# Eight steps of the conditioning product moved from the even mixer to the second feed-forward

## The chip, the cores and the metric

One Trainium2 chip, of which one core runs the kernel. The metric is the device time of one execution in microseconds (us); a kernel's time is the median of its runs. Engines: TensorE (PE, with its weight loads PEld), VectorE (DVE), ScalarE (ACT), GpSimd (POOL), SyncE (SP, which here only issues transfers).

## What is computed

One inference step of a two-layer trunk for a prompt (512 tokens) and eight samples (4 tokens each), 544 columns in all, in the model width 1024. Each layer has a feed-forward, a mixer and a second feed-forward, so there are four feed-forwards, here called first to fourth (`ffn(0)` to `ffn(3)`), an even mixer after the first and an odd mixer after the third. Each of these six parts is conditioned by a shift, a scale and a gate:

```python
mod = (jax.nn.silu(c) @ ada_w[l] + ada_b[l]).reshape(bx, 3, 3, 1, D_MODEL)   # shift, scale, gate of each part
f = _swiglu(_modulate(x, mod[:, 0]), ffn_w_gate[l, 0], ffn_w_up[l, 0], ffn_w_down[l, 0])
x = _layer_norm(ALPHA * x + 0.5 * (1.0 + mod[:, 0, 2]) * f, ln_g[l, 0], ln_b[l, 0])
def _modulate(x, m): return x * (1.0 + m[:, 1]) + m[:, 0]
def _swiglu(h, wg, wu, wd): return (jax.nn.silu(h @ wg) * (h @ wu)) @ wd
```

`ada_w` is 1024 by 9216 in fp32 for each layer. The even mixer is a differential attention of four heads beside an S5 state-space model, with a paged cache for the samples.

## The kernel before

Activations lie with the model width on partitions, 544 columns in two halves of 272. Each weight is split into two fp32r parts (`wh` by ScalarE at L448, `wl` by VectorE at L449), and a projection is three matmuls for each 128 by 128 block (L460, L461, L462).

**The conditioning product** (`ada`, L174; not touched by the diff). The 18 slots of 512 columns of `ada_w[l]` are worked out two slots (a pair, `(l, s)`) at a time, two pairs in one group. A group is eight steps, one for each 128 rows of the input. A step loads four tiles of 128 by 512 (256 KB each, SP's queue, L202) and runs four fp32 products of 32 columns of weights each, side by side in the array (L185; two records for each product, so eight). After the eighth step the result is copied to rows (ScalarE, L211), transposed (TensorE, L213) and added to the bias (VectorE, L217). `ada` is a generator: each `next` puts down one step's loads and the products of the step that lies `lag` steps back. The products are held behind the last projection matmul traced so far:

```python
with self.tc.issue_after(self.last.ins):
    first = product(3, rs[3])
...
raws[n].append(room(F32, f"h{n % 2}{18 + j}"))
```

In the feed-forwards the loaded tiles have eight slots (two steps, `lag` 2), in place of the last hidden tiles, which are not yet in use. In the even mixer they have four slots (one step, `lag` 1), in a pool of their own (`ar`), and a PSUM bank of their own (`ad`).

**A feed-forward** (`ffn`, L377): a first part of 22 hidden blocks `m`, gate and up projection for each half, Silu (L401, ScalarE), the gating multiplication (L402, VectorE) and a split; then a second part with the down projection and the normalisation. In the first part `next(ada)` is called once for each half while `2 <= m < 18` (from `m` = 4 in the first feed-forward). The `fill` argument is the list of pairs. The first feed-forward works out six pairs, the third four, the second and the fourth none.

**The even mixer** (`even_mix`, L1761): the S5 slices (`s5_slice`: products of L1055 and L1064, then of L1087, whose result `yb` and `yT` go out and come back by POOL's queue at L1090 and L1093), then for each of four heads the projections (`even_qk`; POOL copies the samples' columns at L644 and L645), the attention of the head before (`even_head`: scores L660, exponentials L664, transposes L671, copy L673, values L676) and four `next(ada)`. Then the samples' attention (`sample_attn`) in two groups of four samples: keys and values gathered by POOL from the paged cache (`sK` L698, `sV` L704, five slots together), scores L516, exponential L532, transposes L539 to L541, copies L543 and L544, values L549, and at the end a normalisation (L721). Beside it the end of the S5 part (`s5_end`: a gated projection) and the last head. The scale and the shift of a part are combined on POOL (`scale_shift`, L224), the gate too (`gate`, L219).

The order of the instructions on each engine is laid out once, when the kernel is built, by a planner that goes by the order of the program, by priorities and by its own time model; at run time each engine takes its queue in that order.

Of the kernel before, what the change touches and what calls it, by code (L numbers as in the profile page):

```python
# [9 lines left out]
F32 = mybir.dt.float32  # L10
# [16 lines left out]
class Kern:  # L27
# [1733 lines left out]
    def even_mix(self):  # L1761
        nc, D, tc = self.nc, self.D, self.tc
        es = ExitStack()
        pool = lambda n, b, **k: es.enter_context(tc.tile_pool(name=n, bufs=b, reuse_waits="tile", **k))
        self.wide(5, 1)
        self.psum(s5=1, sc=2, mm=2, ps=2, ad=1)
        with es:
            self.qz = pool("s5z", 1)
            self.cm = p1 = pool("ea1", 1)
            p2 = pool("ea2", 2)  # L1770
            q1 = pool("s5a", 1)
            q2 = pool("s5b", 3)
            self.skp = pool("sk", 5)
            pR = pool("ar", 1)
            ada = self.ada([(0, 16), (1, 0), (1, 2), (1, 4)], lambda dt, tag: pR.tile([128, 512], dt, name="ar", tag=tag[0] + tag[2:]), lambda: self.bank["ad"].tile([128, 512], F32, name="ad"), 1)
            self.cmask = self._ld(p1, "cmask")
            self.smask = self._ld(p1, "smask")
            self.o128 = p1.tile([128, 128], F32, name="o128")
            nc.gpsimd.memset(self.o128, 1.0 / 128)
            self.s5_init(q1)  # L1780
            self.even_u(q2)
            self.vt = p1.tile([128, 5, 512], F32, name="vt")
            self.qs = p1.tile([128, 4, 32], F32, name="qs")
            self.ks = p1.tile([128, 4, 32], F32, name="ks")
            self.aoT = p1.tile([128, 4, 512], F32, name="aoT")
            s5 = [self.s5_slice(d, q1, q2) for d in range(4)]
            v = self.vproj(self.vt, D["even_v"], lambda: p2.tile([128, NT], F32, name="qT"), self.ps)
            next(s5[0])
            for _ in v:
                pass  # L1790
            nc.sync.dma_start(D["a_v"][0:512].rearrange("(t p) n -> p t n", p=128), self.vt[:, 0:4])
            nc.sync.dma_start(D["a_v"][512:544], self.vt[0:32, 4])
            qk = {}
            for h in range(4):
                next(s5[h], None)
                if h < 3:
                    next(s5[h + 1])
                qk[h] = self.even_qk(h, p2)
                if h:
                    self.even_head(h - 1, *qk[h - 1], p1, p2)  # L1800
                for _ in range(4):
                    next(ada, None)
            for _ in ada:
                pass
            aos = self.even_sample(p1, p2)
            self.s5_end(q1)
            self.even_head(3, *qk[3], p1, p2)
            self.split(self.xh[:, 0:4, SP:NT], self.xl[:, 0:4, SP:NT], aos)
            for h in range(4):
                self.split(self.xh[:, h, 0:512], self.xl[:, h, 0:512], self.aoT[:, h])  # L1810

        self.psum(mm=4, ps=4)
        self.wide()
# [13 lines left out]
    def run(self):  # L1827
        nc, D = self.nc, self.D
        self.bes, pools = ExitStack(), ExitStack()
        first = self.bes.enter_context(self.tc.tile_pool(name="first", bufs=1, side="right", reuse_waits="tile"))  # L1830
        self.xh, self.xl = [first.tile([128, 8, NT], F32R, name=n) for n in ("xh0", "xl0")]
        self.pp = pools.enter_context(self.tc.tile_pool(name="pp", bufs=1, side="right", reuse_waits="tile"))
        self.s5a = self.pp.tile([128, 48], F32, name="c_s5_a")
        nc.scalar.dma_start(self.s5a, D["s5_a"])
        self.setup()
        self.ada_setup()
        self.s5hp = self.pp.tile([128, 256], F32, name="s5hp")
        nc.scalar.dma_start(self.s5hp, D["s5_par"][:, 512:768])
        gw, early = self.begin()
        self.s5_angles(pools)  # L1840
        self.ffn(0, lambda: self.gate(0, 0, 0.5), lambda: self.to_next(0, self.scale_shift(0, 1, 0)), [(0, s) for s in range(4, 16, 2)], gw, early, self.s5_matrices)
        self.mu, self.rsh = self.const("rw_mu"), self.const("rw_sh")
        xs = self.dr.tile([128, 8, NT], F32, name="xs")
        self.park(xs)
        self.even_mix()
        self.unpark(xs)
        rg = self.gate(0, 1, 1.0)
        GS = self.scale_shift(0, 2, 1)
        self.outproj(D["even_out"], rg, self.to_next(1, GS), (4, 5, 6, 7, 0, 1, 2, 3))
        self.ffn(1, lambda: self.gate(0, 2, 0.5), lambda: self.to_next(2, self.scale_shift(1, 0, 2)), ())  # L1850
        self.ffn(2, lambda: self.gate(1, 0, 0.5), lambda: self.to_next(3, self.scale_shift(1, 1, 3)), [(1, s) for s in range(6, 14, 2)])
        self.park(xs)
        self.odd_mix()
        self.unpark(xs)
        rg = self.gate(1, 1, 1.0)
        GS = self.scale_shift(1, 2, 4)
        self.outproj(D["odd_out"], rg, self.to_next(4, GS))
        self.ffn(3, lambda: self.gate(1, 2, 0.5), lambda: self.to_out(5))
        self.xes.close()
        self.wes.close()  # L1860
        self.banks.close()
# [158 lines left out]
```

## Time and profile before

| | |
|---|---|
| median of 3 runs | 2570.49 us (2568.71 to 2571.3) |
| profiled execution | 2567.64 us, span 2565.8 us |
| TensorE busy | 2442.6 us (95%) |
| VectorE, ScalarE, GpSimd busy | 1232.4, 943.3, 409.0 us |
| data moved by DMA | 318.27 MB, mean 124 GB/s |

Busy time is the time in which an engine has an instruction under way. Ends of matmuls are modelled, so a busy TensorE is not a TensorE at its peak. The granted clock is the share of TensorE's full clock (2.4 GHz) that it got; its two levels are 1.0 and 0.5 (1.2 GHz), values between are means over a stretch. The idle time in front of an instruction stands in square brackets in a timeline, with what ended it.

### The profile page before, as it was taken

The numbers are of one execution on the slowest core, as the hardware profiler recorded it, in microseconds if no ns is written. First come the engines' busy times: TensorE is split into PE (matmuls) and PEld (weight loads), VectorE is DVE, ScalarE is ACT, GpSimd is POOL, SyncE is SP. The second block draws the span as 40 slices with busy tenths as digits, with TensorE's granted clock in tenths as the row PEclk, the third lists the DMA queues.
The fourth block names the chain that finished last, engine by engine and source line by source line (L and its number), as shares of the span: only waits on it lengthen the run. The fifth ranks groups of instructions, "written<-read, shape, count | busy, mean of one in ns | idle before, by whom it ended". The sixth has DMA issues, their size and how long they took to land.

```text
span 2565.8 us, 50682 instructions
## 1 busy us (share of the span) xinstructions
PE 2442.6 (95%) x20338; PEld 2253.4 (88%) x20338; DVE 1232.4 (48%) x2999; ACT 943.3 (37%) x2051; POOL 409.0 (16%) x616
## 2 busy tenths in 40 slices
PE   6999999899899999999999999889999999999996
PEld 4988999897588999999989999878877578999996
DVE  6532356544577333345423334558664567333343
ACT  4322323435555333224323322545422545333222
POOL 1000016411432000031000003312111122000032
PEclk8999999999999999999999999889988999999998
DMA  7666335567632222223562232322322632222221
GB/s 237 203 217 216 113 118 112 188 216 252 222 122 75 87 88 94 80 80 105 173 222 83 85 91 81 103 77 78 92 75 92 211 113 74 87 89 94 80 80 58
DMA packets 184027, 318.27 MB, mean 124 GB/s; under 512 B 38416, under 2 KB 47040, under 8 KB 183664
## 3 DMA queue, kind: packets, MB, share of 16 engines
q1 hardware_dynamic: 172096, 282.52, 34.6%
q0 software_dynamic: 10400, 31.06, 4.1%
q8 instruction: 159, 2.61, 0.4%
q10 hardware_dynamic: 1296, 1.46, 0.2%
q14 instruction: 76, 0.62, 0.1%
HBM read 288.68 MB, written 26.28 MB: 123 GB/s over the span
## 4 chain that ended last, share of the span: by engine, by line
PE 82%; DVE 7%; DMA 4%; ACT 4%; issue 1%; POOL 1%; SPq 1%; ACTq 0%; POOLq 0%; DVEq 0%
PE mm L460 23%; PE mm L462 23%; PE mm L461 22%; PE ps L185 2%; DVE x L347 1%; DMA ar<-in_ada_w 1%; DMA raw<-in_ada_w 1%; ACT t L249 1%; DVE wl L449 1%; PE sc L1178 1%; PE sc L1156 1%; PE ad L185 1%; PE ps L460 1%; PE ps L462 1%; PE ps L461 1%
## 5 line engine op out<-in xcount | busy, mean ns | idle before, releaser
L460 PE MATMUL mm<-xh,wh 128*128 128x272 f32 x3720 | 1089.4, 295 | 35.5 <-ACT xh L250 10.1
L461 PE MATMUL mm<-xl,wh 128*128 128x272 f32 x3720 | 1082.7, 291 | 2.0 <-DVE xl L251 2.0
L462 PE MATMUL mm<-xh,wl 128*128 128x272 f32 x3720 | 1083.0, 292 | 0.8 <-DVE wl L449 0.8
L460 PEld LDWEIGHTS mm<-xh,wh 128*128 128x128 f32 x3720 | 706.0, 190 | 85.2 <-ACT t L401 31.2
L449 DVE TENSOR_TENSOR wl<-raw,wh 128x512 fp32r<-128x512 f32 (+1 forms) x664 | 458.8, 703 | 537.0 <-ACT wh L448 505.0
L461 PEld LDWEIGHTS mm<-xl,wh 128*128 128x128 f32 x3720 | 710.5, 191 | 7.0 <-DVE xl L251 2.5
L462 PEld LDWEIGHTS mm<-xh,wl 128*128 128x128 f32 x3720 | 706.6, 190 | 7.8 <-issue 4.2
L448 ACT ACTIVATE wh<-raw 128x512 fp32r<-128x512 f32 (+1 forms) x664 | 401.5, 618 | 727.6 <-PE mm L461 565.9
L460 PE MATMUL mm<-hh,wh 128*128 128x272 f32 x1280 | 370.4, 289 | 0.0
L462 PE MATMUL mm<-hh,wl 128*128 128x272 f32 x1280 | 370.4, 289 | 0.0
L461 PE MATMUL mm<-hl,wh 128*128 128x272 f32 x1280 | 369.5, 289 | 0.0
L460 PEld LDWEIGHTS mm<-hh,wh 128*128 128x128 f32 x1280 | 241.4, 189 | 0.8 <-issue 0.4
L461 PEld LDWEIGHTS mm<-hl,wh 128*128 128x128 f32 x1280 | 241.2, 188 | 0.4
L462 PEld LDWEIGHTS mm<-hh,wl 128*128 128x128 f32 x1280 | 241.1, 188 | 0.4
L402 DVE TENSOR_TENSOR t<-t,mm 128x272 f32<-128x272 f32 x169 | 73.4, 434 | 279.6 <-ACT t L401 279.4
L401 ACT ACTIVATE t<-mm 128x272 f32<-128x272 f32 x169 | 65.6, 388 | 318.6 <-PE mm L462 318.6
L297 POOL TENSOR_TENSOR sa<-x 128x272 f32<-128x272 f32 x24 | 26.1, 1087 | 907.4 <-DVE x L291 852.0
L291 DVE SCALAR_TENSOR_TENSOR x<-mm,rg,x 128x272 f32<-128x272 f32 (+1 forms) x96 | 45.9, 479 | 171.4 <-PE mm L462 170.7
L466 DVE TENSOR_TENSOR hl<-t,hh 128x272 fp32r<-128x272 f32 x160 | 69.6, 439 | 35.8 <-ACT hh L465 35.3
L465 ACT ACTIVATE hh<-t 128x272 fp32r<-128x272 f32 x160 | 67.5, 426 | 38.5 <-DVE t L402 38.5
L277 POOL TENSOR_TENSOR sq<-sq,t 128x272 f32<-128x272 f32 x60 | 54.7, 926 | 18.1 <-ACT t L276 17.3
L249 ACT ACTIVATE t<-x,S,G 128x272 f32<-128x272 f32 (+1 forms) x80 | 44.5, 589 | 24.1 <-DVE x L348 23.5
(643 smaller groups left out, 2536.6 us busy)
## 6 DMA issues: line engine op xcount, KB each, us to landing
raw<-in_ada_w SPq DMA_DIRECT2D x192, 256.0 KB
raw<-in_wg SPq DMA_DIRECT2D x176, 256.0 KB
raw<-in_wu SPq DMA_DIRECT2D x176, 256.0 KB
raw<-in_wd SPq DMA_DIRECT2D x160, 256.0 KB
ar<-in_ada_w SPq DMA_DIRECT2D x96, 256.0 KB
raw<-in_odd_rw SPq DMA_DIRECT2D x28, 256.0 KB
xs<-x POOLq DMA_DIRECT2D x16, 272.0 KB, 4.0
x<-xs POOLq DMA_DIRECT2D x8, 544.0 KB, 7.8
```

The costliest lines, as they stand in the source:

```text
L185: return nc.tensor.matmul(ps[32 * j:32 * j + 32], self.c32[:, 9 * k:9 * k + 32], r, start=(k == 0), stop=(k == 7))
L249: nc.scalar.activation(t[:, 0:n], x[:, d, c0:pe], AF.Identity, scale=G[:, d, 0:1], bias=S[:, d, 0:1])
L277: G.tensor_tensor(s["q"], s["q"], t, op=A)
L401: self.act = nc.scalar.activation(s, pss[2 * i], AF.Silu)
L402: mul = nc.vector.tensor_tensor(s, s, pss[2 * i + 1], op=ALU.mult)
L448: nc.scalar.activation(wh[:, 0:w], r[:, 0:w], AF.Copy)
L449: (lo or nc.vector).tensor_tensor(wl[:, 0:w], r[:, 0:w], wh[:, 0:w].bitcast(F32), op=ALU.subtract)
L460: nc.tensor.matmul(ps, wh[:, s], mh, start=first, stop=False)
L461: nc.tensor.matmul(ps, wh[:, s], ml, start=False, stop=False)
L462: self.last = nc.tensor.matmul(ps, wl[:, s], mh, start=False, stop=last)
L465: self.nc.scalar.activation(hi, src, AF.Copy)
L466: return (lo_eng or self.nc.vector).tensor_tensor(lo, src, hi.bitcast(F32), op=ALU.subtract)
```

## The change

The even mixer works out two pairs, `(0, 16)` and `(1, 0)`, in place of four, with three calls for each head in place of four. The two pairs `(1, 2)` and `(1, 4)`, the scale and the gate of the third feed-forward, are worked out in the second feed-forward's first part, which had no pairs. The tiles, slots and banks of both places stay as they are.

```diff
@@ even_mix
-            ada = self.ada([(0, 16), (1, 0), (1, 2), (1, 4)], lambda dt, tag: pR.tile(...), lambda: self.bank["ad"].tile(...), 1)
+            ada = self.ada([(0, 16), (1, 0)], lambda dt, tag: pR.tile(...), lambda: self.bank["ad"].tile(...), 1)
...
                 if h:
                     self.even_head(h - 1, *qk[h - 1], p1, p2)
-                for _ in range(4):
+                for _ in range(3):
                     next(ada, None)
@@ run
-        self.ffn(1, lambda: self.gate(0, 2, 0.5), lambda: self.to_next(2, self.scale_shift(1, 0, 2)), ())
+        self.ffn(1, lambda: self.gate(0, 2, 0.5), lambda: self.to_next(2, self.scale_shift(1, 0, 2)), [(1, 2), (1, 4)])
```

## Rows read from the trace of the kernel before

**Rows 1.** The page, part 4: shares of the chain that ended last, by engine.

```profile
PE 82%; DVE 7%; DMA 4%; ACT 4%; issue 1%; POOL 1%; SPq 1%; ACTq 0%; POOLq 0%; DVEq 0%
```

**Rows 2.** Stretches: length, then PE, PEld, DVE, ACT, POOL busy; clock, DMA share, GB/s.

```profile
805.00:1060.00 255.00, 254.90 (x2035) 254.68 (x2034) 99.25 (x194) 88.99 (x187) 0.00 (x0) 1.00 0.28 89
1239.00:1297.00 58.00, 58.00 (x452) 50.10 (x452) 21.77 (x42) 16.17 (x35) 0.00 (x0) 1.00 0.62 205
574.00:646.00 72.00, 71.93 (x559) 56.36 (x562) 35.91 (x106) 36.92 (x87) 12.95 (x30) 1.00 0.76 240
646.00:676.00 30.00, 28.82 (x219) 20.28 (x211) 16.95 (x60) 21.09 (x51) 14.33 (x19) 1.00 0.76 245
676.00:704.00 28.00, 22.41 (x150) 10.96 (x150) 13.97 (x58) 12.63 (x37) 10.67 (x12) 0.88 0.64 216
```

**Rows 3.** Instructions of tile ar: min/median/max ns, first and last start.

```profile
L185 PE MATMUL ad<-ar,c x128: 592/616/1062, 574.5 to 703.4; 128*32 128x512 f32 x128
L202 SPq DMA_DIRECT2D ar<-in_ada_w x96: 327/382/1421, 485.0 to 2032.9; - x96
```

**Rows 4.** Timeline of TensorE at the mixer's end: start, us, line, tiles [idle before].

```profile
647.88 2.00 PE L1087 MATMUL s<-sX,sWc 64*128 64x72 f32 x16
...
679.57 1.71 PE L185 MATMUL ad<-ar,c 128*32 128x512 f32 x8
681.10 1.89 PE L549 MATMUL s<-sV,sPT 128*32 128x512 f32 x16
...
687.21 1.47 PE L185 MATMUL ad<-ar,c 128*32 128x512 f32 x8 [1.75 <-DMA ar<-in_ada_w]
688.61 1.65 PE L676 MATMUL ps<-vt,wT 128*128 128x128 f32 x6
...
695.99 1.07 PE L185 MATMUL ad<-ar,c 128*32 128x512 f32 x8 [0.83 <-DMA ar<-in_ada_w]
...
697.82 1.93 PE L516 MATMUL s<-sK,sq 128*32 128x256 f32 x32
...
702.96 1.07 PE L185 MATMUL ad<-ar,c 128*32 128x512 f32 x8 [1.66 <-DMA ar<-in_ada_w]
```

**Rows 5.** Gating multiplications (L402) of the second, third and fourth feed-forward.

```profile
L402 DVE TENSOR_TENSOR t<-t,mm x42: 429/434/440, 809.6 to 1059.0; 128x272 f32<-128x272 f32 x42
...
L402 DVE TENSOR_TENSOR t<-t,mm x42: 429/434/440, 1219.0 to 1488.6; 128x272 f32<-128x272 f32 x42
...
L402 DVE TENSOR_TENSOR t<-t,mm x42: 429/434/440, 2156.3 to 2406.0; 128x272 f32<-128x272 f32 x42
```

**Rows 6.** Timeline of POOL: start, us, line, tiles.

```profile
669.84 0.22 POOL L645 COPY ks<-kT 128x32 f32<-128x32 f32 x1
...
689.55 0.95 POOL L698 DMA_INDIRECT sK<-in_cak,pidx  x1 [0.31 <-issue]
```

**Rows 7.** Line 698, the gathers of keys: from issue to landing.

```profile
DMA to landing us min/median/max: 4.0/5.4/6.4
```

**Rows 8.** Timelines of ScalarE and of VectorE at the mixer's end.

```profile
684.92 0.49 ACT L673 ACTIVATE wT<-ps 128x384 f32<-128x384 f32 x1 [1.25 <-PE ps L671]
...
704.17 0.66 ACT L211 ACTIVATE row<-ad 128x256 f32<-128x256 f32 x2 [2.27 <-PE ad L185]
704.71 0.51 ACT L532 ACTIVATE sP<-s,sst 128x288 f32<-128x288 f32 x1
...
680.02 0.27 DVE L544 COPY sPT<-s 32x128 f32<-32x128 f32 x1
...
702.40 0.15 DVE L530 TENSOR_SCALAR sst<-sst 128x1 f32<-128x1 f32 x1
```

**Rows 9.** Stretches of 5 us, TensorE alone: length, busy, clock, DMA share, GB/s.

```profile
495.00:500.00 5.00, 2.75 (x20) 1.00 0.00 1
500.00:505.00 5.00, 1.96 (x7) 0.50 0.52 188
725.00:730.00 5.00, 3.08 (x21) 1.00 0.15 21
```

More of the change, by code (lines that the diff above doesn't have):

```diff
@@ L1774, in even_mix @@
             pR = pool("ar", 1)
-            ada = self.ada([(0, 16), (1, 0), (1, 2), (1, 4)], lambda dt, tag: pR.tile([128, 512], dt, name="ar", tag=tag[0] + tag[2:]), lambda: self.bank["ad"].tile([128, 512], F32, name="ad"), 1)
+            ada = self.ada([(0, 16), (1, 0)], lambda dt, tag: pR.tile([128, 512], dt, name="ar", tag=tag[0] + tag[2:]), lambda: self.bank["ad"].tile([128, 512], F32, name="ad"), 1)
             self.cmask = self._ld(p1, "cmask")
```

## The prediction

> **What bounds the kernel now.** I read the page first: TensorE carries 82% of the chain of waits [rows 1], so work of its kind is free only where TensorE waits for something else. Then the table by stretches [rows 2], to see whether the place that loses the work and the place that gets it are such places. In the second feed-forward's first part (805 to 1060) TensorE is busy 254.90 of 255.00 us: no hole. In the even mixer from 574 to 676 it is busy all but 1.25 us; from 676 to 704 it is busy 22.41 of 28 us at a granted clock of 0.88 [rows 2]. The moved work is the second of the mixer's two groups. Its eight steps stand at 645.6, 652.8, 661.4, 671.3, 679.6, 687.2, 696.0 and 703.0 (the timeline of TensorE: the last four are in [rows 4], the first and last start of all 16 steps in [rows 3]), so four of them lie in the full stretch and four in the sparse one. There the question is which wait ends last.
>
> **What the second feed-forward gets.** Eight steps of four products, 32 loads of 256 KB on SP's queue, two row copies on ScalarE, transposes, two additions on VectorE. The third feed-forward carries two such groups in the same loop, with the same banks and the same raw slots; the second and fourth carry none. From the first to the last of the gating multiplications it takes 269.6 us, the other two 249.4 and 249.7 [rows 5]. So two groups cost 20.2 or 19.9 us, one costs **10.0 us**, all on the path, since TensorE has no idle time there. (One step is 1.07 us of products, eight records of some 0.6 us that overlap [rows 3, 4]; the rest is the turn from and to the projections, and the transposes.) The loads: 32 issues of 0.38 us [rows 3] are 12.2 us of SP's queue, put between the loads of the gate and up weights. Behind a late load would stand a product on TensorE, and behind that all projections. In the third feed-forward, where the first group runs, the DMA engines are 0.62 busy and TensorE is still busy 58.00 of 58.00 us [rows 2], so I cost this at nothing; the loads are asked for two steps ahead. If that cover failed, each late load would cost what it costs at the mixer's end, 0.8 to 1.8 us [rows 4]. ScalarE and VectorE, 89 and 99 us busy in 255, hide their few instructions [rows 2]. The values are used by POOL, and POOL does nothing before 1060 [rows 2]. Bounds of this term: 9.9 and 10.1.
>
> **What the even mixer gives back**, from the front to the back.
> First, the full stretch. In the loop each head now gets three calls in place of four, and the products of a head's calls stand behind that head's projections. So ahead of the last S5 slice's second products (647.88 [rows 4]) there were nine steps and one set of transposes; there will be seven steps. Two steps are 2.1 us by their products alone and 2.5 as a quarter of a group's 10.0; the first group's transposes, which now come later, add a little: **2.7 us** earlier. From there the path leaves TensorE: the slice's result goes out and comes back by POOL's queue, whose next gathers hold POOL to 669.84 [rows 6], so the steps at 652.8 to 671.3 give nothing more until the sample attention's first group.
> Second, the step at 679.57 stands ahead of the first group's values (681.10) [rows 4], whose operand is ready at 680.29 (last VectorE copy: 680.02 and 0.27 long [rows 8]). So 0.8 us, in all **3.5**.
> Third, the values free the slots for the second group's keys. POOL issues the last of their gathers at 689.55 [rows 6], which becomes 686.05. They land 4.0 to 6.4 us after issue, median 5.4 [rows 7], so at 691.4. The scores that use them start at 697.82 [rows 4], behind the steps of 687.21 and 695.99, which waited 1.75 and 0.83 us for their loads. Head 3 on the same queue loses that too: its values of 688.61 had their operand by 685.41 (ScalarE's copy, 684.92 and 0.49 [rows 8]) and stood behind the step of 687.21, and so can move by 3.1 more than the 3.5. So the gather is what is late next: 697.82 becomes 691.4, **6.4** in all (5.4 or 7.8 at the landing's ends).
> Fourth, the scores' exponential on ScalarE (704.71) has its operand at 702.55 (VectorE, 702.40 and 0.15) but stands behind the two row copies of the last step, and these behind the step of 702.96 that waited 1.66 us for its load [rows 4, 8]. That is 2.1 us, **8.5** in all. From 705 to the mixer's end nothing of the moved group stands on the path, but for four transposes; the output projection's loads and the reload of x are released by the mixer's end and follow it.
> Bounds: with the gathers' slowest landing 7.5, with the quickest 9.9; if the first part gives nothing, 5.8.
>
> **The sum.** +10.0 − 8.5 = +1.5 us. The profiled execution took 2567.64 us (span 2565.8 and 1.8 around it), so it would take 2569.1; the median of the runs shown is 2.85 above it, so I say 2572.0. Own range of this case: +0.1 to +4.2, that is 2570.6 to 2574.7.
>
> **The rivals.**
> A, *slower: the clock falls in the emptied end*. Place: 676 to 712. TensorE's granted clock was 0.50 (1.2 GHz throughout) from 500 to 505, after 5 us in which it had 2.75 us of work [rows 9]; from 676 to 704 it was 0.88 with the moved steps there [rows 2]. Without their 5.3 us (the four in [rows 4]) the stretch keeps 17.1 us of work in about 22 in place of 22.41 in 28: 0.78 in place of 0.80, which speaks against it, but the work comes in lumps. Price: on the path in that stretch stand products of 5.5 us (L549, L676 and L516 [rows 4]), with the scores between them an estimated 7; at the lower level a step took 1.71 us for 1.07 [rows 4], 1.6 times, so +4; and 2 more if the gate's projections after 704 begin at that level. Net +7.5: 2578. It decides when the mean clock of that stretch falls under about 0.7. The Trainium skill ("TensorE: Matmul & The Clock Gate", Part 1: The HAM clock gate) says that the throttled state is the default and that activity releases it; by that rule taking filler products out of a stretch with holes speaks against this change. The trace agrees with the rule at 500, and shows full clock at 725 to 730 with 3.08 us of work in 5 [rows 9].
> B, *faster: all of it comes back*. The group's 10.0 us, the 4.2 us in which TensorE waited for its loads (1.75, 0.83 and 1.66 [rows 4]), and the 1.0 us that two steps took beyond 1.07 [rows 4] (1.71 and 1.47): 15.2, net −5.2: 2565.3. It needs the gathers to be no bound, by landing sooner once 8.4 MB fewer share the mixer's DMA engines (0.76 busy to 676, 0.64 after [rows 2]). Against it: even the quickest landing leaves 9.9. The Trainium skill ("Trainium Kernel Development and Optimization", Key Constraints) has the queues of SP, ScalarE and POOL share the same 16 DMA engines; by that rule the gathers do gain, and the trace's landings of 4.0 to 6.4 us fit, though no row separates load from latency.
> C, *the mixer's front gives nothing*: the chain over POOL and ScalarE from 650 to 676 starts where it did, because the planner, which lays out the whole mixer anew when a group is gone, uses the room for something else. The gain is 5.8, net +4.2: 2574.7. That is also the form in which the change would not do what it says: TensorE is relieved where it was not what came last.
>
> **How the numbers follow.** This kernel can be told from no change by about 0.2%, 5.1 us: under 2565.4 and over 2575.6. Forecast 0.55, all of it within. A 0.17, nearly all slower. B 0.10, two thirds faster. C 0.18, with the new layout's own spread a quarter of it slower, a fifth faster. That gives faster 0.11, same 0.69, slower 0.20. The range holds the forecast, C and the better half of A, and the upper part of B: 2566.5 to 2577.5.
>
> **What would show it.** In the changed kernel the gating multiplications of the second feed-forward should span 259.4 us (249.4 + 10.0), with TensorE still without idle time; more than 261 means late loads. The mixer's last normalisation (the sample's, after which the output projection starts) should come 8.5 us earlier; 5.8 is C, less with a clock under 0.7 is A, 15 is B. The second group's scores should start close behind the landing of its last gather, with no step ahead of them. I would be wrong if the planner put the gathers elsewhere on POOL's queue, or if the third feed-forward or what follows moved by itself: all from 1060 on should be the same as before but for a shift.

## The result, and the profile after

The change makes the kernel slower. Its median is 2583.85 us (2580.07 to 2590.12), that of the kernel before, run beside it on the same chip, 2570.45 us; the ratio is 1.0057 [1.0045, 1.0068], that is +14.7 us [11.6, 17.5]; the two medians alone lie 13.4 us apart, the figure that some of the texts below use. The profiled execution took 2584.12 us (span 2582.3) at a mean clock of 0.964; before it was 2567.64 us and 0.969. From here on, "us over" is always the ratio less one, times 2570 us, of runs on one chip.

First the place that got the group. The gating multiplications of the second feed-forward (a line's own view: shortest, median and longest in ns, first and last start), the answer to [rows 5]:

```profile
L402 DVE TENSOR_TENSOR t<-t,mm x42: 430/434/440, 812.9 to 1073.8; 128x272 f32<-128x272 f32 x42
```

They span 260.9 us in place of 249.4: +11.5, and TensorE is still without a hole there (265.00 of 265.00 us in the first row below). Then the place that lost it: the table of stretches, to be read against [rows 2] (length, then PE, PEld, DVE, ACT, POOL busy; clock, DMA share, GB/s), and three of the 5 us pieces of the mixer's end:

```profile
808.00:1073.00 265.00, 265.00 (x2105) 257.10 (x2104) 98.60 (x193) 88.57 (x186) 1.32 (x4) 1.00 0.34 109
646.00:676.00 30.00, 27.30 (x202) 20.59 (x201) 15.94 (x57) 21.72 (x47) 13.48 (x19) 0.96 0.49 148
676.00:704.00 28.00, 23.83 (x156) 18.30 (x155) 17.03 (x60) 24.32 (x54) 7.45 (x8) 0.92 0.18 57
...
675.00:680.00 5.00, 5.00 (x20) 3.94 (x19) 2.61 (x9) 4.92 (x10) 0.00 (x0) 0.50 0.00 0
...
715.00:720.00 5.00, 2.33 (x12) 0.88 (x15) 4.79 (x16) 2.46 (x9) 0.96 (x1) 0.50 0.50 161
720.00:725.00 5.00, 5.00 (x23) 0.92 (x15) 2.33 (x5) 2.04 (x5) 0.00 (x0) 0.50 0.15 52
```

From 676 to 704 TensorE is no emptier than before: 23.83 us busy against 22.41. It does other work there. ScalarE has nearly doubled: 24.32 us busy in 28, where it had 12.63 [rows 2]. The timelines of TensorE, ScalarE, POOL and VectorE, one fence each, say what came in (start, us, line, tiles, idle before):

```profile
681.90 0.31 PE L524 MATMUL s<-ks,sq 128*128 128x32 f32 x2
...
692.23 1.92 PE L549 MATMUL s<-sV,sPT 128*32 128x512 f32 x16
...
704.71 3.61 PE L516 MATMUL s<-sK,sq 128*32 128x256 f32 x32 [0.53 <-DMA sK<-in_cak,pidx]
...
718.89 3.64 PE L549 MATMUL s<-sV,sPT 128*32 128x512 f32 x16 [1.76 <-DVE ast L665]
```
```profile
680.34 0.49 ACT L1115 ACTIVATE t<-mm,c_s_glub 128x272 f32<-128x272 f32 x1
681.88 0.49 ACT L1115 ACTIVATE t<-mm,c_s_glub 128x272 f32<-128x272 f32 x1 [1.06 <-PE mm L462]
684.01 0.49 ACT L1115 ACTIVATE t<-mm,c_s_glub 128x272 f32<-128x272 f32 x1 [0.84 <-PE mm L462]
684.52 1.28 ACT L664 ACT_TABLE_LOAD   x1
687.02 0.48 ACT L532 ACTIVATE sP<-s,sst 128x288 f32<-128x288 f32 x1
...
694.93 1.28 ACT L1115 ACT_TABLE_LOAD   x1
```
```profile
701.05 0.95 POOL L698 DMA_INDIRECT sK<-in_cak,pidx  x1 [0.30 <-issue]
```
```profile
684.26 0.15 DVE L530 TENSOR_SCALAR sst<-sst 128x1 f32<-128x1 f32 x1
...
733.46 0.29 DVE L721 TENSOR_SCALAR ssq<-s 128x128 f32<-128x128 f32 x1 [0.57 <-PE s L720]
```

The same three places in the kernel before (TensorE, VectorE, ScalarE):

```profile
673.59 0.31 PE L524 MATMUL s<-ks,sq 128*128 128x32 f32 x2
...
675.40 0.14 DVE L530 TENSOR_SCALAR sst<-sst 128x1 f32<-128x1 f32 x1
...
675.83 0.48 ACT L532 ACTIVATE sP<-s,sst 128x288 f32<-128x288 f32 x1
```

The planner has moved the S5 gate's projections and five of its eight sigmoids (L1115) from after the samples' second scores to before the samples' first exponential. That exponential (L532) now runs at 687.02 in place of 675.83. Most of the delay arises on TensorE: the group's last scores (L524) stand behind the gate's projections, which run in part at the lower clock (0.50 from 675 to 680), so that the exponential's operand (L530) is ready at 684.41 in place of 675.54. ScalarE, with a table load and two exponentials of a head in front, adds 2.6 us. The first group's values (L549) follow at 692.23 in place of 681.10 [rows 4], and the last gather of keys goes out at 701.05 in place of 689.55 [rows 6]. What is left for the end is a thin chain of the samples alone, and there the clock is at its lower level: the scores L516 take 3.61 us for 1.93 [rows 4], the values L549 3.64.

By milestones, each as the distance from the mixer's first instruction (the first parking transfer, L1817, at 501.04 before), with what the prediction forecast; the two right columns belong to experiments below (the change with the order of the kernel before held: k1, and k5 with eight loads moved besides) and stand against another profile of the kernel before (f1):

| us from the mixer's start | before | forecast | change | f1 (before) | k1 | k5 |
|---|---|---|---|---|---|---|
| head 3's copy on POOL, L645 | 168.8 | -2.7 | 169.3 (+0.5) | 168.8 | 167.5 (-1.3) | 166.3 (-2.5) |
| first group's values, L549 | 180.1 | -3.5 | 190.5 (+10.5) | 180.1 | 178.9 (-1.2) | 177.5 (-2.6) |
| last gather of keys, L698 | 188.5 | -3.5 | 199.4 (+10.9) | 188.6 | 189.1 (+0.5) | 187.3 (-1.3) |
| second exponential, L532 | 203.7 | -8.5 | 209.9 (+6.3) | 204.5 | 198.7 (-5.9) | 197.4 (-7.2) |
| last normalisation, L721 | 226.5 | -8.5 | 231.8 (+5.3) | 227.3 | 222.5 (-4.9) | 223.0 (-4.4) |
| first Silu of the next feed-forward | 308.1 | -8.5 | 310.8 (+2.7) | 309.1 | 308.8 (-0.3) | 306.4 (-2.7) |

So the mixer and the output projection gave nothing back; they took 2.7 us more. With 11.5 in the feed-forward, that is the loss. (The change's way from L721 to the first Silu is 2.6 us shorter than before; its output projection's first loads go out at 722.40, 11.1 us ahead of L721, where in f1 they went out at 728.44, 0.9 behind it.)

### The profile page after: what moved, and what is told of

Read it like the earlier page. It is cut to its first block, busy times and chain, and to the rows that moved or that the text cites. A ratio compares the mean times of both kernels' runs of the same rounds, so it can differ in the third digit from the quotient of the medians.

```text
span 2582.3 us, 50662 instructions
## 1 busy us (share of the span) xinstructions
PE 2454.1 (95%) x20338; PEld 2262.9 (88%) x20338; DVE 1231.6 (48%) x2999; ACT 949.5 (37%) x2055; POOL 409.4 (16%) x616
## 4 chain that ended last, share of the span: by engine, by line
PE 82%; DVE 7%; DMA 4%; ACT 3%; issue 2%; POOL 1%; SPq 0%; ACTq 0%; POOLq 0%; DVEq 0%
PE mm L460 23%; PE mm L462 22%; PE mm L461 22%; PE ps L185 2%; DVE x L347 1%; DMA raw<-in_ada_w 1%; DVE wl L449 1%; PE sc L1178 1%; PE sc L1156 1%; ACT t L249 1%; DMA ar<-in_ada_w 1%; PE ps L460 1%; PE ps L462 1%; PE rs L1498 1%; PE ps L461 1%
## 5 line engine op out<-in xcount | busy, mean ns | idle before, releaser
L402 DVE TENSOR_TENSOR t<-t,mm 128x272 f32<-128x272 f32 x169 | 73.4, 434 | 285.4 <-ACT t L401 285.2
L277 POOL TENSOR_TENSOR sq<-sq,t 128x272 f32<-128x272 f32 x60 | 55.2, 934 | 17.3 <-ACT t L276 16.5
L290 POOL TENSOR_TENSOR x<-x,sm 128x272 f32<-128x272 f32 x48 | 50.0, 1071 | 18.8 <-ACT sm L303 18.8
```

Of the source, the lines that this page charges most:

```text
L277: G.tensor_tensor(s["q"], s["q"], t, op=A)
L290: G.tensor_tensor(xd(d), xd(d), s["m"], op=S_)
L402: mul = nc.vector.tensor_tensor(s, s, pss[2 * i + 1], op=ALU.mult)
```

## The experiments

Each kernel was run beside the kernel before on one chip. The table has all of them; the four lengths are from one profiled execution each: the mixer (L1817 to L721), the way from there to the first Silu of the second feed-forward, that feed-forward's first part (first to last Silu), and the odd mixer (last Silu of the third feed-forward to the first of the fourth). Four kernels (e2, e5, g4, k2) leave the group out of both places, so that the scale and the gate of the third feed-forward are zero.

| kernel | ratio [interval] | us over | mixer | to first Silu | first part | odd mixer |
|---|---|---|---|---|---|---|
| before; f1 (the same) | 0.9997 [0.9988, 1.0006] | -0.8 | 226.5; 227.3 | 81.7; 81.8 | 249.1; 249.9 | 668.0; 665.4 |
| the change | 1.0057 [1.0045, 1.0068] | 14.7 | 231.8 | 79.0 | 260.5 | 668.9 |
| e1 getting half | 1.0099 [1.0079, 1.0120] | 25.4 | 236.3 | 86.6 | 260.0 | 671.1 |
| e2 giving half | 1.0017 [1.0002, 1.0031] | 4.4 | 233.3 | 79.0 | 250.5 | 671.0 |
| e3 change, sigmoids held | 1.0053 [1.0035, 1.0072] | 13.6 | 229.9 | 86.9 | 260.8 | 671.8 |
| e4 change, four calls | 1.0065 [1.0047, 1.0084] | 16.7 | 241.3 | 79.1 | 260.7 | 671.5 |
| e5 giving half, sigmoids held | 1.0032 [1.0021, 1.0043] | 8.2 | 233.3 | 78.8 | 250.7 | 666.8 |
| f2 as e3, first loads late | 1.0067 [1.0055, 1.0079] | 17.2 | 227.5 | 83.1 | 259.8 | 671.4 |
| f3 change, first loads late | 1.0066 [1.0054, 1.0078] | 17.0 | 230.0 | 79.0 | 260.5 | 669.3 |
| g1 as e1 | 1.0096 [1.0081, 1.0112] | 24.7 | 228.7 | 84.4 | 259.2 | 670.9 |
| g2 change, idle products | 1.0090 [1.0076, 1.0104] | 23.1 | 235.1 | 78.8 | 260.5 | 672.2 |
| g3 as e3, idle products | 1.0108 [1.0092, 1.0123] | 27.8 | 220.9 | 90.2 | 259.5 | 673.9 |
| g4 as e5, idle products | 1.0000 [0.9991, 1.0009] | 0.0 | 227.0 | 81.8 | 250.2 | 665.2 |
| k1 change, order held | 1.0032 [1.0019, 1.0045] | 8.2 | 222.5 | 86.3 | 260.2 | 665.3 |
| k2 giving half, order held | 1.0005 [0.9996, 1.0014] | 1.3 | 225.0 | 83.8 | 249.4 | 670.2 |
| k3 getting half, order held | 1.0056 [1.0042, 1.0071] | 14.4 | 231.4 | 86.5 | 260.1 | 664.5 |
| k4 as k1, idle products | 1.0037 [1.0023, 1.0051] | 9.5 | 221.8 | 87.0 | 259.5 | 667.8 |
| k5 as k1, first loads late | 1.0026 [1.0014, 1.0037] | 6.7 | 223.0 | 83.5 | 259.7 | 665.2 |
| k6 as k3, first loads late | 1.0053 [1.0037, 1.0069] | 13.6 | 229.3 | 81.5 | 260.2 | 665.1 |

**One half alone.** e1 takes the kernel before and adds the group to the second feed-forward; e2 takes the change and leaves the group out there.

```diff
@@ e1, g1, against the kernel before
-        self.ffn(1, lambda: self.gate(0, 2, 0.5), lambda: self.to_next(2, self.scale_shift(1, 0, 2)), ())
+        self.ffn(1, lambda: self.gate(0, 2, 0.5), lambda: self.to_next(2, self.scale_shift(1, 0, 2)), [(1, 2), (1, 4)])
@@ e2, against the change
+        nc.gpsimd.memset(self.mod(1, 8, 16), 0.0)
-        self.ffn(1, lambda: self.gate(0, 2, 0.5), lambda: self.to_next(2, self.scale_shift(1, 0, 2)), [(1, 2), (1, 4)])
+        self.ffn(1, lambda: self.gate(0, 2, 0.5), lambda: self.to_next(2, self.scale_shift(1, 0, 2)), ())
```


> The even mixer stays as before with both its groups, and the second feed-forward works out the moved group once more: only the receiving half of the change. Its row of the sum was +10.0 us, so 2580.5 against 2570.5. If the 13.4 us of the change all arose in the second feed-forward, this would be 2584; if the second feed-forward had room for the group, 2571.

> Only the giving half of the change: the even mixer with one group and three calls, and nobody works out the scale and the gate of the third feed-forward (left out; they are set to zero once at the start). The sum had -8.5 for this: 2562. Theory of the order (without the group the planner puts the gate's projections of the S5 part ahead of the samples' attention, and that attention then ends the mixer alone on a TensorE at 1.2 GHz): +2 to +5, 2573 to 2576. If the steps were never on the mixer's path and the order did no harm: 2570 to 2571.

Both came out on the wrong side: the giving half alone costs 4.4 us, the getting half 25.4, and the sum of the two (30) is twice the change. Costs of work would add up; these don't. (Beside e1 to e4 the kernel before itself ranged from 2569.6 to 2583.7 us, wider than beside the others; but g1, the kernel of e1 on another chip, is 24.7 us over too.) The feed-forward's own part is as forecast in all kernels that have the group (259.2 to 260.8, against 249.1 to 250.7 without it). What differs lies in the mixers and in the way to the first Silu, where e1 has no instruction that the kernel before has not, but for the group's first loads.

**Single edges.** The sigmoids held behind the second exponential on ScalarE (e3, e5), the old number of calls (e4), and the group's first two steps of loads held behind the feed-forward's first weights on SP's queue (f2, f3).

```diff
@@ e3, e5, f2: the gate's sigmoids behind L532
+                with self.tc.issue_after(self.sexp.ins):
                     nc.scalar.activation(sg, ps, AF.Sigmoid, bias=self.s5gb[:, d:d + 1])
@@ e4
-                for _ in range(3):
+                for _ in range(4):
@@ f2, f3: rawload is the last weight load issued so far
-                    with self.tc.issue_after(load.ins) if j else nullcontext():
+                    with self.tc.issue_after((load if j else self.rawload).ins) if j or n < 2 and pairs[0] == (1, 2) else nullcontext():
```


> The change, with one edge more: the sigmoids of the S5 gate are held on ScalarE behind the exponential of the samples' second group, which is where the planner had put them in the kernel before. Theory of the order: the mixer now gives back what the sum said, 2572, at any rate 2569 to 2577. Rival, the mixer's end was never relieved (chain of gathers on POOL, or the clock, whatever the order): 2580 to 2585 as the change is.

> The change with four calls for each head in place of three, so that the one group that is left stands where it stood before. Theory of the calls (the spread of the remaining steps over the heads displaced the mixer): back to about 2572. Theory of the order: the gate's projections still go first once the second group is gone, so 2580 to 2586.

> Only the giving half (the scale and the gate of the third feed-forward left out, set to zero), with the sigmoids of the S5 gate held behind the second group's exponential as in the kernel before. Without the hold it was 4.4 us slower than before. Theory of the order: -8.5, at any rate -4 or better. Rival, the group was never on the path of the mixer's end: +2 to +6 as without the hold.

> The change with the hold, and with the first two steps' loads of the moved group held on SP's queue behind the gate and up weights of the block at which their step is called, so that none of them stands among the output projection's loads. Theory of the loads (eight loads of 256 KB ahead of the output projection's last weights cost 4 to 8 us there, which the sum had at nothing): 5 us less than the change with the hold alone, which was +13.7, so +6 to +9. If the loads cost nothing: +13.7 again.

> The change with the late loads alone, without the hold. Theory of the loads: +13.4 less what they cost in the change's own order, where they stand behind ten of the thirteen last output projection loads, 1 to 5 us: +9 to +12. If the loads cost nothing: +13 to +15.

> The kernel before itself, once more, for its profile on the same chip as the runs beside it: 0 against before, within 0.2%. If the mixer takes the same 727.5 us to its last normalisation as in the profile of before, the longer mixers seen in the other kernels are theirs; if it is 8 to 10 us longer here too, they belong to the chip.

None of them is the cause by itself: 13.6, 16.7, 8.2, 17.2 and 17.0 us over. The mixer alone runs from 227.5 to 241.3 us in these kernels, and in e3 and f2 what it lost less, the way to the first Silu lost more (86.9 and 83.1). In e3 the first group's values still stand at 187.7 us from the mixer's start (180.1 before), so the sigmoids on ScalarE were not what held them up. The edges of e3, e4 and e5 make the planner lay out the mixer, the output projection and even the odd mixer anew, so each of these runs changes more than its edge. The late loads don't: f3 has the order of the change on TensorE, VectorE, ScalarE and POOL, instruction for instruction, and f2 that of e3 but for ten records. So f3 tests the late loads alone, and they gain nothing in the change (17.0 against 14.7, intervals that overlap). Against e3, f2 has a way that is 3.8 us shorter, but not a shorter time (17.2 against 13.6). f1 shows what the measurement itself leaves: 0.8 us.

**Idle products under the planner's order.** Rival A's theory was that the removed products had kept the clock up. So four fp32 products of the same form, on the resident `vt` and with a result that nobody reads, were put at five places of the mixer's end (the texts say six; the trace of g2 has 40 records, five steps of eight).

```diff
+    def fill(self, anchor, h=0):
+        with self.tc.issue_after(anchor.ins), self.tc.high_priority(offset=4000):
+            for j in range(4):
+                self.nc.tensor.matmul(self.filled[32 * j:32 * j + 32], self.c32[:, 0:32], self.vt[:, j], start=True, stop=True)
```


> The kernel before, with the second feed-forward working out the scale and the gate of the third feed-forward a second time; the mixer keeps both groups and, up to the output projection, its order of instructions on every engine. It was run once beside a kernel before that itself scattered by 14 us; it is measured again. If the group costs its 10.1 us in the feed-forward and nothing else, the time is 10 to 12 us over that of the kernel before, and the mixer's last normalisation (L721) comes within 1.5 us of its old distance from the mixer's start. If the loads of the first two steps, asked for in the output projection, cost something of their own, it is 14 to 18 us, and the stretch from L721 to the first Silu of the second feed-forward is over 84 us (81.6 before).

> The change, with six steps of idle work put into the mixer's end on TensorE: each four fp32 products of the form of the moved ones (128 by 512, 32 columns of weights), on values that are resident, so with no loads, and with a result that nobody reads. Two stand beside the scores of the third block of head 2, one behind the first group's transposes, one behind the first group's output, one behind the second group's last scores of new keys. The theory that the removed products had kept the clock up expects 8 to 11 us over the kernel before (the feed-forward's 10, the mixer at or under its old length), a granted clock over 0.85 from 675 to 715 and the second group's scores (L516) at about 1.9 us in place of 3.6. The theory that the planner's new order alone is to blame, with the sigmoids of the S5 gate ahead of the samples' attention, expects 13 to 15 us as for the change, since that order stays, whatever the clock.

> As the run before, with the sigmoids of the S5 gate held behind the second group's exponential besides, so that the gate's projections stand behind the samples' attention as in the kernel before. The change with the hold alone took 17 us over the kernel before beside late loads, and 14 us without. If clock and order both count, this is the best of the forms: 6 to 10 us over the kernel before, the mixer 0 to 4 us shorter than before. If neither does, because the mixer's end is a chain of latencies over other engines and queues, 13 to 17 us.

> The giving half alone, with the hold and the six steps of idle work: the group is in neither place, so that the scale and the gate of the third feed-forward are zero. Without the idle work this took 8.2 us over the kernel before. The clock's theory expects 0 to 6 us under the kernel before, as the mixer has lost its loads and its waits and keeps the clock. The theory of the order, or of a chain of latencies, expects 5 to 9 us over it, as without the idle work.

g4 (0.0, where e5 had 8.2) looks like proof for the clock; g2 and g3 (23.1 and 27.8, worse than without the idle products) look like proof against it. g3 is the instructive one: its mixer is 6.4 us shorter than f1's, of 8.5 that were forecast, and its way to the first Silu 8.4 us longer. And g1, whose order of instructions up to L721 is that of the kernel before, is 24.7 us over. With the order free, nothing can be told apart.

**The order held.** So the order was taken out of the question. Every instruction that the kernel before and the new kernel have in common was chained to its predecessor in the order in which the kernel before has it, on all five engines; the group's own instructions, and the small POOL steps that need its result, are free. The calls for each head are four again, so that the first group's steps keep their places.

```diff
+def held(tc, nc):
+    traced = nc.cur_bb.bb.instructions
+    for code in ORDER.values():
...
+        line = [traced[k] for k in np.cumsum(steps, dtype=np.int64)]
+        for a, b in zip(line, line[1:]):
+            tc.add_manual_dep(b, a.name, mybir.DependencyInfo(mybir.DependencyClass.NoSync, mybir.DependencyReason.DATA), reason="order")
```


> The change, with every instruction that both kernels have held in the order in which the kernel before has it, engine by engine, by order edges (with four calls for each head, so that the first group's steps keep their places); only the moved group's own instructions and the four small steps on GpSimd that need its result are free. The sum of the prediction (+10.0 in the feed-forward, -8.5 in the mixer) took the order as fixed: if it was right but for the new layout, this kernel is 0 to 4 us over the kernel before, and the odd mixer takes what it took. If the clock is the cause, the mixer still gives back little: 7 to 14 us over, with the second group's scores and values at the lower level in some stretch between 670 and 740. If the output projection's loads are held up by the group's first loads, the stretch from the mixer's last normalisation (L721) to the first Silu is over 84 us (81.6 before).

> The giving half alone with the order of the kernel before held: the group is in neither place (the scale and the gate of the third feed-forward are zero). The sum expects 8.5 us under the kernel before (6 to 10). The clock's theory expects 0 to 8 us over it, as for the giving half without the held order (4 and 8 us over). A chain of latencies that the products never stood on expects no change, within 2 us.

> The getting half alone with the order held: the mixer keeps both groups and the second feed-forward works out the second one again. Without the held order this took 24 us over the kernel before, of which its first part shows 10 to 11, the odd mixer 5 to 6 and the way to the first Silu 4. If the odd mixer's part came from its new order, it is gone here, and the time is 10 to 15 us over. If it came from the group by itself (its loads, or a clock that it disturbs), it stays: 18 to 24 us.

> The first of these four with the second group's products kept in the mixer, at their old places, as idle work: on values that are resident, with no loads, no row copies, and a result that nobody reads. Against that run it adds 32 products and nothing else. The clock's theory expects it faster than that run by 3 to 8 us, with a granted clock from 675 to 715 at or over that of the kernel before. The sum, which has the products on the path, expects it slower by 3 to 5 us (the steps at 645 to 653 and at 680). If neither counts, the two are the same within 2 us.

k1 is 8.2 us over [4.9, 11.6]; the change was 14.7 [11.6, 17.5] on another chip. The intervals just meet. Two closer pairs say the same: k1 differs from e4 by the held order alone (16.7 [12.1, 21.6] with the order free), and k3 from e1 and g1 (14.4 [10.8, 18.2], against 25.4 [20.3, 30.8] and 24.7 [20.8, 28.8]). Some 6 to 10 us are thus the planner's new order. The remaining 8 are the group's 10 with almost nothing given back. In the mixer itself the forecast chain is there: the second exponential comes 5.9 us earlier (column k1 of the first table), the last normalisation 4.9. Then it is lost: the first Silu stands 0.3 us before its old place. k2 says the same without the group: mixer 2.4 us shorter, first Silu 0.3 earlier, time unchanged (1.3 us [-1.0, 3.6]). The halves still don't add up, though: k2 and k3 together are 15.7 us over, k1 8.2. Against k3, on the same chip, k1 is 6.2 us faster and its mixer 8.9 us shorter; against the kernel before it gains little. That gap is open (see below).

k4 against k1 asks for the clock: only 32 idle products differ. The table of stretches, k1 first and then k4:

```profile
665.00:675.00 10.00, 8.41 (x45) 5.62 (x45) 7.04 (x30) 9.88 (x22) 4.32 (x5) 1.00 0.66 200
675.00:690.00 15.00, 13.29 (x52) 6.16 (x53) 8.02 (x28) 5.45 (x19) 3.78 (x4) 0.53 0.16 41
690.00:705.00 15.00, 11.92 (x81) 7.97 (x80) 9.91 (x44) 11.53 (x30) 8.96 (x11) 0.84 0.58 167
```
```profile
675.00:690.00 15.00, 13.77 (x75) 5.79 (x74) 9.58 (x34) 7.69 (x25) 2.18 (x3) 0.77 0.07 19
690.00:705.00 15.00, 12.64 (x98) 6.68 (x94) 8.87 (x41) 10.38 (x27) 9.23 (x11) 1.00 0.60 169
```

In k1 the clock is at the lower of its levels (0.5, 1.2 GHz) almost throughout 675 to 690, after TensorE had 8.41 us of work in the 10 before 675 (f1, with the group's products there: 9.02). These pieces alone don't tell the kernels apart: k5, with k1's order and no idle products, has 0.77 from 675 to 690 too, and k2 has 0.96 from 690 to 705. The whole end of the mixer does (TensorE alone; k1, k2, k5, then k4):

```profile
675.00:715.00 40.00, 35.21 (x198) 0.74 0.33 93
675.00:715.00 40.00, 34.86 (x188) 0.74 0.34 93
675.00:715.00 40.00, 34.03 (x198) 0.79 0.33 93
675.00:715.00 40.00, 36.36 (x240) 0.91 0.33 93
```

So the idle products bring the clock back (f1 has 0.87). The time doesn't notice: k4's mixer is 0.7 us shorter than k1's, the first Silu stands 308.73 and 308.75 us from the mixer's start, and the ratios are 1.0037 and 1.0032. As far as one profile each can say, that is a balance and not a clock without effect: k4's first values come 2.1 us later than k1's (181.0 and 178.9 us from the mixer's start), and from them to L721 it takes 2.8 us less (40.8 and 43.6). So k4 does not price the clock by itself; it shows that idle products are no remedy. The Trainium skill ("TensorE: Matmul & The Clock Gate", Part 1: The HAM clock gate) has the throttled state as the default which activity releases. These kernels agree with that, with 0.91 for k4 and 0.74 to 0.79 for k1, k2 and k5.

**The first loads.** In k1 and k3 the planner has put the group's first eight loads between the 13 loads of the output projection, in the change behind ten of them. SP's queue of the change, of k1, and of k5, where they are held behind the feed-forward's first weights (the edge of f2 and f3):

```profile
722.40 19.54 SPq L446 DMA_DIRECT2D raw<-in_even_out  x10
743.08 3.65 SPq L202 DMA_DIRECT2D raw<-in_ada_w  x8
748.06 2.69 SPq L446 DMA_DIRECT2D raw<-in_even_out  x3
```

```profile
725.89 12.76 SPq L446 DMA_DIRECT2D raw<-in_even_out  x6
739.93 1.75 SPq L202 DMA_DIRECT2D raw<-in_ada_w  x4
741.78 0.85 SPq L446 DMA_DIRECT2D raw<-in_even_out  x2
742.68 0.43 SPq L202 DMA_DIRECT2D raw<-in_ada_w  x1
743.20 0.38 SPq L446 DMA_DIRECT2D raw<-in_even_out  x1
743.63 2.27 SPq L202 DMA_DIRECT2D raw<-in_ada_w  x3
748.67 5.99 SPq L446 DMA_DIRECT2D raw<-in_even_out  x4
```
```profile
725.62 24.21 SPq L446 DMA_DIRECT2D raw<-in_even_out  x13
751.63 1.40 SPq L446 DMA_DIRECT2D raw<-in_wg  x2
...
788.08 3.67 SPq L202 DMA_DIRECT2D raw<-in_ada_w  x8
```


> The change with the order held, as k1, and the group's first eight loads held behind the loads of the feed-forward's first gate and up weights on SP's queue, so that the output projection's 13 loads stand together as in the kernel before. If those loads ate the mixer's gain, the stretch from L721 to the first Silu falls from 86.3 to about 82 us and the kernel is 3 to 6 us over the kernel before (k1: 8.7). If the output projection is held up by its own loads and the reload of x, it stays at 7 to 11 us over.

> The getting half alone with the order held, as k3, with the same eight loads moved back. If the loads are the cause of what k3 took beyond the group's own 10 us, this is 9.5 to 12 us over the kernel before (k3: 16.4), and the stretch from L721 to the first Silu is 81 to 83 us (k3: 86.5). If not, 14 to 18 us.

(These texts count by the difference of the medians: 8.7 for k1 and 16.4 for k3, 8.2 and 14.4 by the ratio.) The way from L721 to the first Silu shrinks by 2.8 us in k5 (86.3 to 83.5) and by 5.0 in k6 (86.5 to 81.5, the old length). In k1 the chain of waits runs over three late loads, which are gone from k5's:

```profile
727.10 9.76 DMA raw<-in_even_out
...
741.78 5.49 DMA raw<-in_even_out
...
748.67 4.20 DMA raw<-in_even_out
...
754.34 3.20 DMA raw<-in_even_out
```

So in the profiles the loads cost that much at their place, in these two pairs and in e3 and f2 (86.9 to 83.1). The times don't confirm it: k5 is 1.5 us under k1 and k6 0.8 under k3, both within their intervals and on different chips, and f2 is 3.6 over e3. k5 is the best form of the change, and at 6.7 us over it is still slower than the kernel before. No kernel tried here beats that one.

## Why the prediction was wrong

**The feed-forward's term was right.** +10.0 was forecast. From the first to the last gating multiplication the fourteen kernels with the group take 259.5 to 261.1 us, 260.4 on average, and the six without it 249.4 to 251.0, 250.3 on average: 10.1 us. For a single kernel the bounds of 9.9 and 10.1 were too narrow: the change is 11.5 over before, k1 10.3 and k5 9.8 over f1 (250.2). The change shows no idle time of TensorE there, as forecast.

**"I cost this at nothing" (the loads) failed.** They were weighed in the place where they are used, the feed-forward's first part, where the DMA engines have room. But the first two steps are asked for two steps ahead, which is in the output projection, among loads that TensorE is waiting for: by the profiles 2.8 us in k5 against k1, 5.0 in k6 against k3. The prediction noted that they are asked for two steps ahead, and didn't walk SP's queue back to where the first of them would then stand. In the change itself the planner put them behind ten of the thirteen (at 743.08), and there they cost nothing: f3, with them late, has the same 79.0 us.

**The mixer's term failed at its root: the sum took the order of the instructions as fixed.** All four of its steps read what would start earlier if the products vanished from a given queue. The queue wasn't given. The planner lays out the mixer again, and pulled the gate's projections and sigmoids into the freed room; the first exponential came 10.5 us later behind them, and with it everything that hangs on it. The gathers of the second group came 10.9 us later where 3.5 earlier was forecast, and L721 5.3 us later where 8.5 earlier was forecast. This was rival C in its form (the planner uses the room for something else), but sized there as a gain of 5.8 in place of 8.5, and not as a loss. The first step also miscounted: it left seven steps ahead of the last S5 slice's second products (L1087), and the change has all eight there, the last one right in front (TensorE of the change):

```profile
649.00 1.07 PE L185 MATMUL ad<-ar,c 128*32 128x512 f32 x8 [0.19 <-DMA ar<-in_ada_w]
650.00 2.00 PE L1087 MATMUL s<-sX,sWc 64*128 64x72 f32 x16
```

**With the order held, the steps can be read one by one** (first table, k1 and k5). But with four calls for each head these kernels keep all eight steps and the transposes (L213) ahead of that slice, so that one step is gone there and not two. TensorE of k1:

```profile
644.21 0.60 PE L213 MATMUL ad<-c_cst,row 128*128 128x128 f32 x4
...
649.21 2.00 PE L1087 MATMUL s<-sX,sWc 64*128 64x72 f32 x16
```

By the prediction's own prices (1.1 to 1.25 us for a step) its steps then stand at an estimated 1.2, 2.0 and 7.0 us in place of 2.7, 3.5 and 8.5. The front: 1.3 and 2.5 us of 1.2. The first values: 1.2 and 2.6 of 2.0; they run at the lower clock, 3.64 and 3.25 us for 1.89 [rows 4], which is rival A at its place.

```profile
681.40 3.64 PE L549 MATMUL s<-sV,sPT 128*32 128x512 f32 x16 [0.75 <-PE s L541]
696.14 1.93 PE L516 MATMUL s<-sK,sq 128*32 128x256 f32 x32
```

(TensorE of k1.) The second exponential: 5.9 and 7.2 of 7.0, so that "the gather is what is late next" and the waits for the group's own loads were right in kind and, as far as one profile each can tell, in size. (Head 3's values could move by 3.2 more, and not 3.1: 688.61 less 685.41. Nothing hangs on it.) From there on the prediction said that the path follows unchanged, and it doesn't: between that exponential and the second values f1 takes 9.8 us, k1 10.8 and k5 12.6, with the clock at 0.92 (k1, the first row) and 0.79 (k5, the second) from 705 to 715, where f1 has 1.00. The others fit: k2 takes 12.6 at 0.72, k4 9.8 at 1.00.

```profile
705.00:715.00 10.00, 10.00 (x69) 6.53 (x69) 4.28 (x14) 7.96 (x16) 0.74 (x1) 0.92 0.22 59
```
```profile
705.00:715.00 10.00, 10.00 (x63) 6.59 (x62) 4.46 (x14) 6.19 (x12) 0.00 (x0) 0.79 0.04 14
```

**"The output projection's loads and the reload of x ... follow it" was the last step to fail**: of the 4.4 to 4.9 us that reach L721, 2.7 reach the first Silu in k5 and 0.3 in k1; of k2's 2.4, 0.3. In k2 and k5, where none of the group's loads are in the way, the stretch is 1.7 to 2.0 us longer than in f1. And k1, k2 and k4 reach the first Silu 308.7 to 308.8 us from the mixer's start, though their L721 lies at 222.5, 225.0 and 221.8. The chains of k2 and k5 run over the landing of the first output weights (9.85 and 9.59 us, f1 8.67), then over the split of those weights and head 3's last copy on ScalarE, with the clock at 0.66 from 740 to 745 where f1 has 1.00. Which of these takes the 2 us was not tried apart.

**The rivals.** A's condition, a mean clock under about 0.7 from 676 to 704, is met in k1 (0.68) and not in the change (0.92), whose clock is low from 675 to 680 and after 704. A's price of 1.6 times was too low: the step at 679.57 ran only in part at the lower level (0.68 from 679 to 682), and products wholly at it took 1.9 times (L549: 3.64 us for 1.89). The sign of the result is A's, but k4 has the clock back and is no faster. What the clock costs in the change's own order was not separated, since g2, meant for that, got another order. B is out: in no kernel did more than 2.7 us come back at the first Silu. Its premise did show: the last six gathers of keys land 3.4 to 4.1 us after issue in k1, for 4.0 to 4.6 before and 3.5 to 6.6 in f1 (the median of 5.4 in [rows 7] is over all gathers of the line). C had the right mechanism and the wrong size. "All from 1060 on should be the same but for a shift" was wrong too: the odd mixer is laid out anew in most kernels. But its time can't be charged to the change: with one and the same order it takes 664.5 to 671.0 us (k1 to k6, before, f1, e2), and the change's 668.9 lies among these.

**What stays open.** The kernels that keep both groups in the mixer and so have, up to L721, the very order of the kernel before but for four small POOL steps (e1, g1, k3, k6) all have a longer mixer: 228.7 to 236.3 us, where two profiles of the kernel before have 226.5 and 227.3. No instruction explains it, and it is most of what k6 shows beyond 10. So what the mixer gives back depends on the twin: k1 and k5 have mixers that are 8.9 and 6.3 us shorter than those of k3 and k6, but 4.9 and 4.4 shorter than f1's. The loss of the change itself is accounted for by place (11.5 in the feed-forward, 2.7 up to it, 0.9 in the odd mixer, of 16.5 between the two profiled spans), but how much of it is the planner's order, 6 to 10 us, rests on ratios from different chips.

## What to carry to other kernels

Where a planner lays out a stage, taking work away is not a subtraction: before a stall is booked as a gain, ask what the planner will pull into the hole, and to test a cause, hold the order and vary the work. A gain at the end of a stage counts at the next stage's first result, so follow it through the loads and copies that start there. Loads that are asked for ahead are priced where they are issued, among that place's loads, and not where their data is used.

## What the runs showed of the hardware

One and the same order of instructions can differ from profile to profile by more than the effect under study: the odd mixer of f1 and of k2, instruction for instruction in the same order, takes 665.4 and 670.2 us (the table of stretches over the whole odd mixer, f1 first, then k2):

```profile
1489.70:2155.10 665.40, 618.91 (x6065) 535.75 (x6064) 386.29 (x1034) 272.56 (x623) 150.03 (x269) 0.94 0.32 99
```
```profile
1490.30:2160.50 670.20, 620.30 (x6061) 537.84 (x6060) 387.66 (x1034) 272.91 (x623) 149.06 (x269) 0.93 0.32 98
```

The work is the same to 1.4 us; 3.4 us are idle time of TensorE, and the mean clock differs by 0.01. So a single profile settles a place to some 5 us here, sometimes worse: the even mixer of e1 and g1, one kernel in one order, takes 236.3 and 228.7 us. Only medians of several runs settle the time. The lower clock level was dear for single operations (L549: 3.64 us for 1.89) and cheap for the whole: 40 us at 0.74 in k1 against 0.91 in k4 moved the mixer's end by 0.7 us, while the idle products that raised the clock had made the first values 2.1 us later.
